# The last products of an encoder layer accumulate on banks that hold x and the gated sums

## The chip, the cores and the metric

The kernel runs on one core of one Trainium2 chip. The core has five engines with queues of their own: TensorE (PE, its weight loads PEld), VectorE (DVE), ScalarE (ACT), GpSimd (POOL) and SyncE (SP), which here only issues transfers. TensorE writes its results to PSUM, eight banks of 512 float32 columns by 128 partitions. The metric is the device time of one execution in microseconds, lower is better; runs are compared by their median.

## The reference

One layer of an encoder on 512 tokens of width 1024. After a norm and a projection to eight parts of 1024 columns there are a recurrent branch (convolution, two gated scans) and an attention branch over a neighbourhood of the token grid; both go through a projection, a gate each, and a sum. The end of the layer is what the change is about:

```python
merged = jax.nn.sigmoid(ga) * y_a + jax.nn.sigmoid(gb) * y_b
x = x + gate[:, None, :] * (merged @ w_o[l])
...
y = x32 * lax.rsqrt(jnp.mean(x32 * x32, axis=-1, keepdims=True) + EPS)   # rms_norm(x, g_final)
return (y * g.astype(jnp.float32)).astype(x.dtype)
```

`gate` is one row of 1024 numbers for all tokens, `w_o` is 1024 x 1024, and the output is float32.

## The kernel before

**Precision.** A float32 product is made of three TensorE products of a rounded high part and a low part (`mm3`: high by high, high by low, low by high), which accumulate in one bank. So each operand is split first: ScalarE writes the high part (`cast`, L411), VectorE subtracts it for the low part (`sub`, L414).

**The middle.** 72 main projections of 192 matmuls each (64 block products in three parts, 128x512 results called `acc`) follow each other on TensorE. Between their matmuls lie those of the attention (`sp`, `pt`, `pv`; VectorE makes `pp` from `pt` at L837, and `pv` multiplies `pp` by `vt`) and of the scans' gates (`gt`, 64 rows deep).

**The last stage.** `merged @ w_o` is done as a block product with seven instead of eight products (`ORDER`): merged is cut into quarters (token halves by halves of the inner dimension), `w_o` into the quarters 11, 12, 21, 22. Each product has sums of quarters on both sides: on the left `a11`, `a12`, `a22`, `s1` to `s4`; on the right 11, 21, 22 and `t1` to `t4` (`SUMS`; signs lie on the left side and in the sums afterwards). The inner half is four blocks of 128, so each product has for each of two token tiles t (0 and 1) 4 x 3 = 12 matmuls of 128x512, into a bank called `st`. The results are then combined: sums u1, u2, u3, and from them the four quarters of the output. A tile t of the upper half and tile t + 2 of the lower half share products; the output rows lie in `yo`, `y[t, n]` is the half row n of tile t. x is loaded into `yo` first.

Operations here before the change: the product 11 gives u1 (ScalarE copies the bank); u1 times gate is added to x in `yo`; u2 = u1 + t2's product, u3 = u2 + t3's; c22 and c12 from t1's; c21 = u3 + t4's; c12 + 22's product; each is multiplied by gate and added to `yo` (`mix`, L1131; sums with a bank at L1288); the product 21, with the gate already in its right side, is added to `yo` at L1284. Then `part_done`: squares of `yo` with a row sum (ScalarE L1234, in the very last piece VectorE L1230), the row's sums (L1242, L1243), root (ScalarE L1248), v, reciprocal and a Newton step (VectorE L1249 to L1254), the product with `gfin` (L1237, VectorE or GpSimd) and with the row's factor (ScalarE L1264 for a whole row of 1024; in the last tile VectorE L1258 and ScalarE L1261 for a half each), and the stores (L1265, L1260, L1262).

**Staging of w_o.** The 28 right sides (7 sums, 4 inner blocks) are made while the projections run: SP loads one quarter's block into `wb` (L406), GpSimd issues transfers that add the other quarters (`woa`, L1200), ScalarE and VectorE split it, SP writes it to a buffer in DRAM (`wscr`, L1208), and in the last stage it is loaded again as `woh`. `POS` says for each of the 28 behind which projection this starts. For the sum 21 the block is loaded into `wr` instead and multiplied by gate before it is split.

**What sets the order.** Every instruction is recorded by `op` with an engine, or a choice of them, a cost, and a rank; a planner (`Plan`) then runs a list schedule with these costs, with slots for each pool of tiles and with a limit on live banks of each kind (`LIMITS`), and emits each engine's instructions in that order. At run time each engine goes strictly in its order and waits for semaphores. So a change of any rank, cost or position shifts the order elsewhere too.

Of the kernel before, what the change touches and what calls it, by code (L numbers as in the profile page):

```python
# [348 lines left out]
def layer(ctx, tc, x, x_t, cin, par, w_m, w_v, w_vt, w_in, w_blk, rpb, w_pa, w_pb, w_o, g_final, out):  # L349
# [17 lines left out]
    def T(name, dt=F32):  # L367
        return pl.tile("s", lambda i: sb.tile([P, S], dt, tag=f"s{i}", name=nm(name)))
# [47 lines left out]
    def mm(o, a, b, first, last):  # L416
        nc.tensor.matmul(o, a, b, start=first, stop=last)  # L417
# [771 lines left out]
    for k in range(4):  # L1189
        block = {f"{i}{j}": w_o[(k + 4 * i - 4) * P:(k + 4 * i - 3) * P, 512 * j - 512:512 * j] for i in (1, 2) for j in (1, 2)}  # L1190
        for j, (_, g) in enumerate(ORDER):
# [31 lines left out]
    def part_done(t, n, a, b, rank, o, last, final):  # L1223

        w = b - a
        yy = lambda: yo[t].ap[:, n * 512 + a:n * 512 + b]
        rows = slice(t * P, (t + 1) * P)
        ssq = C("ssq", 1, 10)
        if final and last:
            op("DVE", dve(w) + 0.08, lambda e: nc.vector.tensor_tensor_reduce(  # L1230
# [188 lines left out]
```

## Time and profile before

| | |
|---|---|
| runs | 550.95, 552.49, 550.82 us; median 550.95 |
| profiled execution | 549.81 us, its span 548.0 us, granted TensorE clock 0.996 |
| busy, share of the span | PE 537.1 us (98%), PEld 447.0 (82%), DVE 419.7 (77%), ACT 343.4 (63%), POOL 131.4 (24%) |
| transfers | 132.35 MB, 241 GB/s over the span |
| the chain that ended last | PE 92%, DVE 4%, DMA 2% |

A line of the timeline gives start, duration, engine, source line, operation, output <- inputs, shape and count; in brackets stands how long the engine had been idle and what ended that. Neighbouring instructions of one kind are put together in one line, with their count. The duration of a matmul is longer than the distance to the next, because matmuls are pipelined. A line of the groups gives source line, engine, operation, names, shape and count, then total busy time and mean of one in ns, then the idle time before them. A line of the waits says who waited for whom, the sum, how often, and the longest.

### The profile page before, as it was taken

How to read it: one execution, taken by the hardware profiler on the slowest of the kernel's cores; microseconds unless marked ns; L12 is line 12 of the kernel's file. 1: busy time of each engine (PE TensorE's matmuls, PEld its weight loads, DVE VectorE, ACT ScalarE, POOL GpSimd, SP SyncE). 2: the span in 40 equal slices, each digit the busy share in tenths (PEclk: the TensorE clock that was granted, in tenths of full speed). 3: DMA queues.
4: the chain of work that ended last, by engine and by line, in shares of the span. 5: the costliest groups of instructions: out<-in, count | busy, mean ns of one | idle time of the engine just before them, and what ended most of it. 6: DMA issues, size and time to landing. Idle time of an engine off the chain costs nothing.

```text
span 548.0 us, 7826 instructions
## 1 busy us (share of the span) xinstructions
PE 537.1 (98%) x2684; PEld 447.0 (82%) x2684; DVE 419.7 (77%) x772; ACT 343.4 (63%) x614; POOL 131.4 (24%) x100
## 2 busy tenths in 40 slices
PE   9999999999999999999999999999999999999993
PEld 8888888888888888887887888888788888888882
DVE  5679518898788789888768988986974884688486
ACT  5578645854864755776986984996698535334044
POOL 3528656444433534220000000000002011000052
PEclk9999999999999999999999999999999999999998
DMA  8999999888976794487173174232319979999933
GB/s 329 408 409 407 368 343 332 227 309 254 253 238 241 189 317 125 126 198 221 43 306 135 39 225 158 98 109 85 115 45 320 303 228 282 348 390 415 413 154 154
DMA packets 48544, 132.35 MB, mean 241 GB/s; under 512 B 6512, under 2 KB 9720, under 8 KB 48504
## 3 DMA queue, kind: packets, MB, share of 16 engines
q1 hardware_dynamic: 44168, 124.18, 63.2%
q0 software_dynamic: 4032, 7.34, 7.7%
q8 instruction: 21, 0.34, 0.3%
q10 hardware_dynamic: 304, 0.33, 0.2%
q14 instruction: 19, 0.16, 0.1%
HBM read 110.69 MB, written 21.14 MB: 241 GB/s over the span
## 4 chain that ended last, share of the span: by engine, by line
PE 92%; DVE 4%; DMA 2%; ACT 0%; SPq 0%; issue 0%; DVEq 0%; ACTq 0%
PE acc L417 70%; PE hx L417 8%; PE st L417 5%; PE pv L417 2%; PE gt L417 2%; PE sp L417 2%; PE pt L827 2%; DMA rcx<-rscr 2%; DVE v L1249 1%; DVE yo L1131 1%; PE hx L526 1%; SPq L406 0%; PE mi L463 0%; DVE u L1131 0%; DVE u L1288 0%
## 5 line engine op out<-in xcount | busy, mean ns | idle before, releaser
L417 PE MATMUL acc<-hhl,whi 128*128 128x512 f32 x784 | 242.9, 391 | 0.0
L417 PEld LDWEIGHTS acc<-hhl,whi 128*128 128x128 f32 x784 | 145.8, 188 | 29.9 <-issue 0.4
L417 PE MATMUL acc<-hhl,wlo 128*128 128x512 f32 x392 | 152.7, 390 | 0.0
L417 PEld LDWEIGHTS acc<-hhl,wlo 128*128 128x128 f32 x392 | 73.6, 188 | 15.5
L1200 POOL DMA_DIRECT2D wb<-in_w_o_dram x28 | 24.4, 879 | 257.1 <-DMA wb<-in_w_o_dram 222.5
L414 POOL TENSOR_TENSOR wlo<-wraw,whi 128x1024 fp32r<-128x1024 f32 x27 | 67.6, 2512 | 74.1 <-ACT whi L411 58.2
L411 ACT CAST whi<-wraw 128x1024 fp32r<-128x1024 f32 x72 | 74.6, 1046 | 7.6 <-DMA wraw<-in_w_in_dram 4.5
L414 DVE TENSOR_TENSOR wlo<-wraw,whi 128x1024 fp32r<-128x1024 f32 x45 | 55.4, 1233 | 5.9 <-ACT whi L411 5.6
L417 PE MATMUL acc<-yahl,whi 128*128 128x512 f32 x128 | 39.4, 389 | 0.0
L417 PE MATMUL acc<-ybhl,whi 128*128 128x512 f32 x128 | 39.4, 389 | 0.0
L816 ACT ACTIVATE p<-p,mn 128x192 f32<-128x192 f32 (+1 forms) x64 | 30.4, 478 | 6.3 <-DVE mn L809 6.2
L809 DVE CUSTOM_DVE_ANT_0 p<-sp,nb 128x192 f32<-128x192 f32 (+1 forms) x64 | 31.0, 603 | 0.4
L417 PEld LDWEIGHTS acc<-ybhl,whi 128*128 128x128 f32 x128 | 24.0, 188 | 5.0
L417 PEld LDWEIGHTS acc<-yahl,whi 128*128 128x128 f32 x128 | 24.0, 188 | 5.0
L969 DVE SCALAR_TENSOR_TENSOR xc<-acc,prm,xc 128x511 f32<-128x511 f32 (+1 forms) x24 | 18.0, 749 | 12.3 <-ACT xc L962 11.8
L1063 DVE SCALAR_TENSOR_TENSOR gm<-gm,acc 128x512 f32<-128x512 f32 x16 | 11.0, 687 | 21.1 <-PE acc L417 21.1
L417 PE MATMUL acc<-ybhl,wlo 128*128 128x512 f32 x64 | 24.9, 389 | 0.0
L417 PE MATMUL acc<-yahl,wlo 128*128 128x512 f32 x64 | 24.9, 389 | 0.0
L1058 ACT ACTIVATE gm<-acc 128x512 f32<-128x512 f32 x16 | 9.6, 598 | 24.4 <-PE acc L417 24.3
L417 PE MATMUL hx<-vhl,xhl 128*128 128x512 f32 x96 | 24.3, 391 | 0.2 <-ACT xhl L567 0.2
L414 DVE TENSOR_TENSOR wb<-wb 128x512 fp32r<-128x512 f32 x24 | 20.4, 864 | 4.6 <-ACT wb L411 4.6
L996 ACT ACTIVATE ri<-gt,hb 64x512 f32<-64x512 f32 x32 | 21.9, 685 | 1.8 <-PE gt L417 1.2
(207 smaller groups left out, 1011.0 us busy)
## 6 DMA issues: line engine op xcount, KB each, us to landing
wraw<-in_w_in_dram SPq DMA_DIRECT2D x56, 512.0 KB
wscr<-wb SPq DMA_DIRECT2D x28, 512.0 KB
woh<-wscr SPq DMA_DIRECT2D x28, 512.0 KB
wc<-in_w_m_dram SPq DMA_DIRECT2D x24, 512.0 KB
wb<-in_w_o_dram POOLq DMA_DIRECT2D x28, 256.0 KB, 7.0
wb<-in_w_o_dram SPq DMA_DIRECT2D x24, 256.0 KB
vt<-vscr SPq DMA_DIRECT2D x20, 256.0 KB
wv<-in_w_v_dram SPq DMA_DIRECT2D x8, 512.0 KB
```

The lines of the kernel that those rows point to most:

```text
L411: return lambda e: nc.scalar.copy(o(), i()) if e == "ACT" else nc.vector.tensor_copy(o(), i())
L414: return lambda e: ENGINE[e].tensor_tensor(o(), a(), b().bitcast(F32), op=ALU.subtract)
L417: nc.tensor.matmul(o, a, b, start=first, stop=last)
L526: op("PE", 0.43, lambda e: nc.tensor.matmul(wb.ap[:, :P], warmc.ap, warmc.ap, start=True, stop=True), 5000 + j, r=[warmc], hold=[wb], unti ...
L809: nc.vector.tensor_tensor_reduce(out=o, in0=v(spv(h, e)[:, :nk]), in1=v(nb[:, h, :nk]), scale=-1.0, scalar=3e38, op0=ALU.add, op1=ALU.min, ...
L816: nc.scalar.activation(pv2(i), pv2(i), AF.Exp, bias=mn.ap[:, c:c + 1], scale=-1.0, accum_out=sm.ap[:, 4 * h + b:4 * h + b + 1])
L827: nc.tensor.transpose(ptp.ap[:, j * P:(j + 1) * P], pt_.ap[:, j * P:(j + 1) * P], ident.ap)
L969: nc.vector.scalar_tensor_tensor(a, b, wcol, a, op0=ALU.mult, op1=ALU.add)
L996: nc.scalar.activation(ri[2 * d].ap[H[e], :], bk[e].ap[H[e], :], AF.Tanh, bias=hb.ap[H[e], c:c + 1], scale=0.5)
L1058: op("ACT", act(512), lambda e: nc.scalar.activation(t.ap, o.ap, AF.Tanh, scale=0.5), n - 1.9, r=[o], w=[t], name="gm")
L1063: op("DVE", dve(512), lambda e: nc.vector.scalar_tensor_tensor(t.ap, t.ap, 1.0, o.ap, op0=ALU.add, op1=ALU.mult), n - 1.9, r=[o], rw=[t], ...
L1200: op("POOL", 1.1, lambda e, l=l, q=q, block=block: nc.gpsimd.dma_start(f32(l)(), block[q], accum_op=ALU.add), m0 + 2, rw=[l], late=6.0, fa ...
```

## The change

It changes the following, nothing else of what the kernel computes:

- **Banks that hold the rest of the sum.** Each tile keeps three banks through the last stage. On the first, the product 11 is copied out (u1) and gated into `v`; VectorE then writes v + x into the bank, and the product 21 accumulates on it (`start=False`, `on`). On the second, t2's product: VectorE adds u1 into the bank, ScalarE copies it out as u2, t3's product accumulates on it, ScalarE copies that as u3, VectorE gates it and writes gated + x into the bank, t4's product accumulates. On the third, t1's: c22 and c12 are read from it, c12 is gated, VectorE writes gated + x into the bank, 22's product accumulates. Only the half row of c22 is finished in `yo`.
- **Squares and scale read the bank.** `square` reads the bank (or `yo` for c22), `scaled` multiplies bank, row factor and `gfin` in one VectorE operation into `yo`. GpSimd keeps only the two products u times gate (c22) in this stage.
- **Gate in 12 operands.** The right sides 21, 22 and t4 are all multiplied by gate while they are staged (12 blocks instead of 4; all in `wr`, where the quarters are also added).
- **Order.** `SEQ` gives the order of the 14 products (number of the product in `ORDER`, plus 7 for tile 1), the last one is whole; `POS` is new; reloads are ranked by `SEQ`; x is loaded some projections sooner; `st` may have eight banks instead of six.

```diff
+SEQ = [0, 7, 9, 2, 8, 6, 1, 10, 3, 4, 12, 5, 11, 13]
+GATED = {"21": 0, "22": 1, "t4": 0}
-LIMITS = {"st": 6, ...
+LIMITS = {"st": 8, ...
...
-    def mm(o, a, b, first, last):
-        nc.tensor.matmul(o, a, b, start=first, stop=last)
+    def mm(o, a, b, first, last, on=False):
+        nc.tensor.matmul(o, a, b, start=first, stop=last, skip_group_check=on)
...
-            raw = T("wr") if g == "21" else None
+            raw = T("wr") if g in GATED else None
...
-            if g == "21":
-                op(EITHER, both(512), lambda e, raw=raw: mix(e, whole(raw), whole(raw), whole(gate[0]), ALU.mult), m0 + 1.5, r=[gate[0]], rw=[raw], lock=True,
+            if raw:
+                gr = gate[GATED[g]]
+                op(EITHER, both(512), lambda e, raw=raw, gr=gr: mix(e, whole(raw), whole(raw), whole(gr), ALU.mult), m0 + LOWR - 0.1 + 0.5 * len(more), r=[gr], rw=[raw], lock=True,
...
-        load(yo[t], whole(yo[t]), x[t * P:(t + 1) * P, :], n1 + 0.2 * t, 524288, after=gate_of(n1, 1), spare=1, name="xr")
+        load(yo[t], whole(yo[t]), x[t * P:(t + 1) * P, :], n1 - 3 + 0.7 * t, 524288, after=gate_of(n1, 3), spare=1, name="xr")
...
+        op("ACT", act(512, 0, True), lambda e: nc.scalar.activation(to.ap, o.ap, AF.Square, accum_out=ssq.ap), rank,
...
+        op("DVE", dve2(512) if 0 else dve(512), lambda e: nc.vector.scalar_tensor_tensor(y[t, n].ap, o.ap, rs.ap, gfin[n].ap, op0=ALU.mult, op1=ALU.mult),
...
+    first_of = {"11": 0, "t2": 1, "t3": 1, "t4": 1, "t1": 2, "22": 2, "21": 0}
+    turns = [(int(c) % 7, int(c) // 7) for c in SEQ]
...
+        grow = (t, first_of[sb_]) in banks
+        o = banks.setdefault((t, first_of[sb_]), None) or B("st")
...
+                mm3(o.ap, ah.ap[:, ts], al.ap[:, ts], bh.ap, bl.ap, k == 0 and not grow, k == 3, grow)
...
+        if sb_ == "11":
+            us[t], v = kept("u1"), T("v")
+            two_of(v, o, gate[0], ALU.mult, "eg")
+            two_of(o, v, y[t, 0], ALU.add, "e0", 0.2)
+        elif sb_ == "t2":
+            two_of(o, us[t], o, ALU.add, "u2")
+            us[t] = kept("u2")
...
+            two_of(c12, c12, gate[1], ALU.mult, "eg", 0.1)
+            two_of(o, w, c12, ALU.add, "e0", 0.2)
...
+        elif sb_ == "t4":
+            part_done(t + 2, 0, o, rank, False)
```

**How it moves instructions.** Source lines below are those of each kernel; a number behind a name tells tiles of one name apart, and x3 are the three parts of one block product.

TensorE at the end of the program, before: the last matmuls of tile 1's product 21, whose second operand is the pair `mhl`. `st_5349` is the product 21 of tile 0, `st_5371` and `st_5390` are the two halves of tile 1.

```order
L417 MATMUL st_5349<-woh_5199,mhl_5040 128x512 x3
L417 MATMUL st_5349<-woh_5209,mhl_5092 128x512 x3
L417 MATMUL st_5371<-woh_5183,mhl_4936 128x256 x3
L417 MATMUL st_5371<-woh_5192,mhl_4978 128x256 x3
L417 MATMUL st_5371<-woh_5199,mhl_5040 128x256 x3
L417 MATMUL st_5371<-woh_5209,mhl_5092 128x256 x3
L417 MATMUL st_5390<-woh_5183,mhl_4936 128x256 x3
```

TensorE at the same place in the new order: `st_5150` is the second bank of tile 1 (t4's product), `st_5122` its first bank, on which 21's product accumulates.

```order
L419 MATMUL st_5150<-woh_5143,mhl_5003 128x512 x3
L419 MATMUL st_5150<-woh_5157,mhl_5057 128x512 x3
L419 MATMUL st_5150<-woh_5168,mhl_5109 128x512 x3
L419 MATMUL st_5122<-woh_5019,mhl_4951 128x512 x3
L419 MATMUL st_5122<-woh_5044,mhl_5003 128x512 x3
L419 MATMUL st_5122<-woh_5262,mhl_5057 128x512 x3
L419 MATMUL st_5122<-woh_5055,mhl_5109 128x512 x3
```

Behind it: one group of 24 half-wide matmuls has become one of 12 whole ones, into a bank that already holds v + x, and t4's product of the same tile is now the one before it.

VectorE at the end of the program, before: `yo_5065` is the row block of tile 1, the names with 128x1 are the row's numbers.

```order
L1284 TENSOR_TENSOR yo_5065<-yo_5065,st_5371 128x256
L1243 TENSOR_SCALAR ssp_5418<-ssq_5406 128x1
L1237 TENSOR_TENSOR yo_5065<-yo_5065,gfin_4301 128x512
L1242 TENSOR_TENSOR ssp_5424<-ssp_5418,ssq_5420 128x1
L1284 TENSOR_TENSOR yo_5065<-yo_5065,st_5390 128x256
L1230 ISA junk_5428,ssq_5427<-yo_5065 128x256
L1230 ISA ssq_5427 128x1
L1249 TENSOR_TENSOR v_1063_5431<-ssq_5427,ssp_5424 128x1
L1250 RECIPROCAL r_1065_5435<-sd_1064_5433 128x1
L1253 SCALAR_TENSOR_TENSOR q_1066_5437<-r_1065_5435,v_1063_5431 128x1
L1254 SCALAR_TENSOR_TENSOR rs_1067_5438<-q_1066_5437,r_1065_5435 128x1
L1258 SCALAR_TENSOR_TENSOR yo_5065<-yo_5065,rs_1067_5438,gfin_4297 128x512
```

VectorE at the same place in the new order: `yo_5071` is the row block of tile 3, `yo_4957` that of tile 1.

```order
L1236 SCALAR_TENSOR_TENSOR yo_4943<-st_5091,rs_1054_5381,gfin_4592 128x512
L1255 TENSOR_TENSOR v_1057_5396<-ssq_5388,ssp_5305 128x1
L1256 RECIPROCAL r_1058_5402<-sd_1056_5394 128x1
L1259 SCALAR_TENSOR_TENSOR q_1059_5404<-r_1058_5402,v_1057_5396 128x1
L1260 SCALAR_TENSOR_TENSOR rs_1060_5405<-q_1059_5404,r_1058_5402 128x1
L1236 SCALAR_TENSOR_TENSOR yo_5071<-st_5150,rs_1060_5405,gfin_4592 128x512
L1236 SCALAR_TENSOR_TENSOR yo_5071<-yo_5071,rs_1060_5405,gfin_4698 128x512
L1255 TENSOR_TENSOR v_1063_5418<-ssq_5413,ssp_5336 128x1
L1256 RECIPROCAL r_1064_5420<-sd_1062_5416 128x1
L1259 SCALAR_TENSOR_TENSOR q_1065_5422<-r_1064_5420,v_1063_5418 128x1
L1260 SCALAR_TENSOR_TENSOR rs_1066_5423<-q_1065_5422,r_1064_5420 128x1
L1236 SCALAR_TENSOR_TENSOR yo_4957<-st_5122,rs_1066_5423,gfin_4592 128x512
```

Behind it: the two adds from a bank (L1284), the square (L1230) and the product with `gfin` (L1237) are gone from this place; the last operation takes the bank `st_5122` directly, and ahead of the last row's numbers stand the two scales of tile 3.

TensorE at a group of `pv` matmuls near 117 us of the profile, before:

```order
L417 MATMUL acc_1296<-hhl_722,whi_1020 128x512 x2
L417 MATMUL acc_1296<-hhl_722,wlo_1030 128x512
L417 MATMUL acc_1296<-hhl_712,whi_1020 128x512 x2
L417 MATMUL acc_1296<-hhl_712,wlo_1030 128x512
L417 MATMUL pv_1343<-pp_1293,vt_757 128x256
L417 MATMUL pv_1343<-pp_1293,vt_764 128x256
L417 MATMUL pv_1344<-pp_1293,vt_757 128x256
L417 MATMUL pv_1344<-pp_1293,vt_764 128x256
L417 MATMUL pv_1343<-pp_1318,vt_764 128x256
L417 MATMUL pv_1343<-pp_1318,vt_771 128x256
```

The same group in the new order, where `acc_1347` is the projection behind `acc_1297`:

```order
L419 MATMUL acc_1297<-hhl_712,whi_1020 128x512 x2
L419 MATMUL acc_1297<-hhl_712,wlo_1030 128x512
L419 MATMUL acc_1297<-hhl_736,whi_1020 128x512 x2
L419 MATMUL acc_1297<-hhl_736,wlo_1030 128x512
L419 MATMUL acc_1347<-hh_602,whi_1103 128x512
L419 MATMUL acc_1347<-hl_618,whi_1103 128x512
L419 MATMUL acc_1347<-hh_602,wlo_1129 128x512
L419 MATMUL pv_1358<-pp_1295,vt_757 128x256
L419 MATMUL pv_1358<-pp_1295,vt_764 128x256
L419 MATMUL pv_1359<-pp_1295,vt_757 128x256
L419 MATMUL pv_1359<-pp_1295,vt_764 128x256
```

What moved: `pv` stands three block rows later, behind `hhl_736` of its own projection and the first three matmuls of the next; six more matmuls of 512 columns lie ahead of it.

TensorE at the first group of gate matmuls (`gt`), near 252 us of the profile, before:

```order
L417 MATMUL gt_2913<-xl_2771,gwh_2421 128x512
L417 MATMUL gt_2912<-xh_2664,gwl_2451 128x512
L417 MATMUL gt_2913<-xh_2664,gwl_2451 128x512
L417 MATMUL pv_2924<-pp_2886,vt_2172 128x256
L417 MATMUL pv_2924<-pp_2886,vt_2181 128x256
L417 MATMUL pv_2925<-pp_2886,vt_2172 128x256
L417 MATMUL pv_2925<-pp_2886,vt_2181 128x256
L417 MATMUL pv_2924<-pp_2891,vt_2181 128x256
L417 MATMUL pv_2924<-pp_2891,vt_2186 128x256
L417 MATMUL pv_2925<-pp_2891,vt_2181 128x256
L417 MATMUL pv_2925<-pp_2891,vt_2186 128x256
L417 MATMUL gt_2941<-xh_2664,gwh_2421 128x512
```

The same place in the new order:

```order
L419 MATMUL acc_2881<-hhl_712,wlo_2678 128x512
L419 MATMUL acc_2881<-hhl_736,whi_2663 128x512 x2
L419 MATMUL acc_2881<-hhl_736,wlo_2678 128x512
L419 MATMUL gt_2940<-xh_2676,gwh_2424 128x512
L419 MATMUL gt_2941<-xh_2676,gwh_2424 128x512
L419 MATMUL gt_2940<-xl_2703,gwh_2424 128x512
L419 MATMUL gt_2941<-xl_2703,gwh_2424 128x512
L419 MATMUL gt_2940<-xh_2676,gwl_2455 128x512
L419 MATMUL gt_2941<-xh_2676,gwl_2455 128x512
L419 MATMUL gt_2954<-xh_2676,gwh_2424 128x512
```

What moved: `pv` no longer lies inside the group (it stands 12 matmuls of `acc` sooner), and all 24 `gt` matmuls of this group follow each other, where before they came as 6, then 8 of `pv`, 12, then 9 of `acc`, and 6. The next groups are whole in both orders, except for the fourth: 24 in a row before, and now 18, then 18 of `acc`, and 6.

More of the change, by code (lines that the diff above doesn't have):

```diff
@@ L1218, in layer @@
         y[t, 0], y[t, 1] = two_in(yo[t])
-        load(yo[t], whole(yo[t]), x[t * P:(t + 1) * P, :], n1 + 0.2 * t, 524288, after=gate_of(n1, 1), spare=1, name="xr")
+        load(yo[t], whole(yo[t]), x[t * P:(t + 1) * P, :], n1 - 3 + 0.7 * t, 524288, after=gate_of(n1, 3), spare=1, name="xr")
     junk = T("junk")
     ssum = {}
-    def part_done(t, n, a, b, rank, o, last, final):
-        w = b - a
-        yy = lambda: yo[t].ap[:, n * 512 + a:n * 512 + b]
-        rows = slice(t * P, (t + 1) * P)
-        ssq = C("ssq", 1, 10)
-        if final and last:
-            op("DVE", dve(w) + 0.08, lambda e: nc.vector.tensor_tensor_reduce(
-                out=junk.ap[:, :w], in0=yy(), in1=yy(), scale=1.0, scalar=0.0, op0=ALU.mult, op1=ALU.add, accum_out=ssq.ap), rank,
-               r=[y[t, n]], w=[ssq, junk], lock=True)
-        else:
-            op("ACT", act(w, 0, True), lambda e: nc.scalar.activation(o.ap[:, :w], yy(), AF.Square, accum_out=ssq.ap), rank,
-               r=[y[t, n]], rw=[o], w=[ssq])
-            if not final or n:
-                op(ANY, any_(w), lambda e: ENGINE[e].tensor_tensor(yy(), yy(), gfin[n].ap[:, a:b], op=ALU.mult),
-                   rank + 0.1, r=[gfin[n]], rw=[y[t, n]], lock=True, name="e2")
-        if not last:
-            p = ssum.get(t)
-            ssum[t] = q = C("ssp", 1, 10)
-            op("DVE", 0.16, (lambda e: nc.vector.tensor_tensor(q.ap, p.ap, ssq.ap, op=ALU.add)) if p else
-               (lambda e: nc.vector.tensor_scalar(q.ap, ssq.ap, D * EPS, None, op0=ALU.add)), rank, r=[ssq] + [p] * bool(p), w=[q])
@@ new lines, in square, with scaled @@
+    def square(t, n, o, rank):
+        ssq = C("ssq", 1, 10)
+        to = junk if o is y[t, n] else y[t, n]
+        op("ACT", act(512, 0, True), lambda e: nc.scalar.activation(to.ap, o.ap, AF.Square, accum_out=ssq.ap), rank,
+           r=[o], w=[ssq] + [to] * (to is junk), rw=[to] * (to is not junk), name="sqy")
+        return ssq
+    def scaled(t, n, o, rs, rank):
+        op("DVE", dve2(512) if 0 else dve(512), lambda e: nc.vector.scalar_tensor_tensor(y[t, n].ap, o.ap, rs.ap, gfin[n].ap, op0=ALU.mult, op1=ALU.mult),
+           rank, r=[rs, gfin[n]] + [o] * (o is not y[t, n]), rw=[y[t, n]], lock=o is y[t, n], name="out")
@@ new lines, in part_done @@
+    def part_done(t, n, o, rank, final):
+        rows = slice(t * P, (t + 1) * P)
+        ssq = square(t, n, o, rank)
+        if t not in ssum:
+            q = C("ssp", 1, 10)
+            op("DVE", 0.16, lambda e: nc.vector.tensor_scalar(q.ap, ssq.ap, D * EPS, None, op0=ALU.add), rank, r=[ssq], w=[q], lock=True)
+            ssum[t] = q, o
+            if final:
+                op("DVE", dve(512), lambda e: nc.vector.tensor_tensor(y[t, n].ap, o.ap, gfin[n].ap, op=ALU.mult), rank + 0.1,
+                   r=[o, gfin[n]], rw=[y[t, n]], name="e2")
@@ L1252, in newton @@
+        op("DVE", 0.17, lambda e: nc.vector.reciprocal(r.ap, sd.ap), rank, r=[sd], w=[r], lock=True)
         def newton(e):
```

130 lines of the change are left out of this document (57 added, 73 removed).

## The prediction

> **What bounds the kernel now.** I read the stretches first, then TensorE's waits, then the end in order of time. One line of the stretches is: from and to in us, length, busy time of PE, PEld, DVE, ACT and POOL (with instructions), granted clock, DMA share, GB/s. The cuts are at 8.6 us (start-up over), 500.5 us (first matmul of the last product) and 539 us (last matmul).
>
> ```profile
> 8.60:500.50 491.90, 491.23 (x2456) 407.83 (x2457) 383.89 (x693) 324.07 (x576) 118.14 (x83) 1.00 0.72 239
> 500.50:539.00 38.50, 38.41 (x181) 32.11 (x179) 28.31 (x53) 11.75 (x25) 9.43 (x7) 1.00 0.74 299
> 539.00:548.00 9.00, 0.00 (x0) 0.00 (x0) 4.40 (x16) 2.83 (x7) 0.65 (x1) 0.77 0.30 117
> ...
> PE hx L526 <- DVE warmc L435: 1.1, 1, 1.1
> PE pv L417 <- DVE pp L837: 0.5, 1, 0.5
> PE hx L417 <- ACT xhl L567: 0.2, 1, 0.2
> ```
>
> TensorE bounds it: busy 491.23 of 491.90 us and 38.41 of 38.50 at full clock. Its only waits are the last three lines, and one of them, 0.5 us for pp, lies where the change moves instructions. So time can come from three places: work that TensorE drops, that wait, and the 9.00 us after TensorE's last matmul. Everything that is taken off VectorE before 539 is worth nothing by itself; it is worth what it takes off the end. The end, in order of time:
>
> ```profile
> 533.16 5.75 PE L417 MATMUL st<-woh,mhl 128*128 128x512 f32 x36
> ...
> 537.39 1.13 DVE L1131 TENSOR_TENSOR yo<-yo,u 128x512 f32<-128x512 f32 x1
> 538.31 1.34 POOL L1237 TENSOR_TENSOR yo<-yo,gfin 128x512 f32<-128x512 f32 x1 [0.34 <-ACT st L1234]
> 538.44 1.23 DVE L1249 TENSOR_TENSOR v<-ssq,ssp 128x1 f32<-128x1 f32 x1
> 538.55 0.60 ACT L1234 ACTIVATE st<-yo 128x512 f32<-128x512 f32 x1
> 539.09 0.19 ACT L1234 ACTIVATION_READ_ACCUMULATOR st<-yo 128x1 f32 x1
> ...
> 540.11 0.41 DVE L1284 TENSOR_TENSOR yo<-yo,st 128x256 f32<-128x256 f32 x1
> ...
> 541.17 0.41 DVE L1284 TENSOR_TENSOR yo<-yo,st 128x256 f32<-128x256 f32 x1
> 541.62 0.42 DVE L1230 CUSTOM_DVE_ANT_0 junk<-yo 128x256 f32<-128x256 f32 x1
> ...
> 542.09 0.16 DVE L1249 TENSOR_TENSOR v<-ssq,ssp 128x1 f32<-128x1 f32 x1
> 542.09 0.29 ACT L1248 ACTIVATE sd<-ssq,ssp 128x1 f32<-128x1 f32 x1
> 542.42 0.16 DVE L1250 RECIPROCAL r<-sd 128x1 f32<-128x1 f32 x1 [0.17 <-ACT sd L1248]
> ...
> 543.06 0.75 DVE L1258 SCALAR_TENSOR_TENSOR yo<-yo,rs,gfin 128x512 f32<-128x512 f32 x1
> ...
> 543.84 0.33 SPq L1260 DMA_DIRECT2D out_dram<-yo  x1
> ```
>
> TensorE ends at 533.16 + 5.75 = 538.91, but the add of its last half starts at 541.17: VectorE is 2.26 us late. It was made late by its queue of 512-wide adds, and by GpSimd: the tiny v took 1.23 us beside a GpSimd product and 0.16 alone, an add took 1.13. After the add come the squares, the root, the scale (543.06), the store (543.84) and 4.16 us to the span's end at 548.0.
>
> **Part 1, the end.** Removed: the adds of x, of the gated sums and of the product behind the last matmuls; the bank then holds the finished row, ScalarE squares it there, VectorE scales it from there. Also the last product is one of 512 columns instead of two of 256. Prices:
>
> ```profile
> 522.28 5.60 PE L417 MATMUL st<-woh,mhl 128*128 128x512 f32 x24
> ...
> 527.72 5.60 PE L417 MATMUL st<-woh,s 128*128 128x512 f32 x24
> 527.92 0.69 DVE L1288 TENSOR_TENSOR u<-u,st 128x512 f32<-128x512 f32 x1 [0.80 <-PE st L417]
> ...
> 538.04 0.19 ACT L1234 ACTIVATION_READ_ACCUMULATOR st<-yo 128x1 f32 x1
> 538.26 0.29 ACT L1248 ACTIVATE sd<-ssq,ssp 128x1 f32<-128x1 f32 x1
> ...
> L1288 DVE TENSOR_TENSOR u<-u,st 128x512 f32<-128x512 f32 x8 | 5.5, 683 | 4.6 <-PE st L417 4.6
> L1131 DVE TENSOR_TENSOR u<-u,gate 128x512 f32<-128x512 f32 x4 | 2.8, 690 | 0.1
> L1234 ACT ACTIVATE st<-yo 128x512 f32<-128x512 f32 x7 | 4.2, 600 | 22.5 <-DVE yo L1131 21.1 <-DVE yo L1284 1.3
> L411 ACT COPY u<-st 128x512 f32<-128x512 f32 x2 | 1.2, 589 | 1.8 <-PE st L417 1.8
> ```
>
> - Matmuls of 512 columns follow each other every (527.72 - 522.28) / 24 = 0.227 us. The last 36 (12 whole, 24 halves) took 5.75; as 24 whole ones they take 5.60: TensorE ends 0.15 sooner, at 538.76.
> - VectorE began 0.04 after a group's end (522.28 + 5.60 = 527.88, then 527.92). ScalarE's square so starts at 538.80. Square and read-out take 539.09 + 0.19 - 538.55 = 0.73, the root follows 0.03 later (538.23 to 538.26): 539.56.
> - Root to scale is kept: 543.06 - 542.09 = 0.97, so the scale starts at 540.53. Scale to store is kept: 0.78, so 541.31. Store to end is kept, 4.16: **545.47 instead of 548.0, a gain of 2.53**.
>
> A square that reads a bank and writes SBUF has the nearest row in the copy out of a bank, 589 ns, against 600 for the square now; a scale that reads a bank has the add u<-u,st, 683 ns, against 690 without a bank. I take both as they are now. [...]
>
> Unknown is a VectorE write into a bank. Reading one costs nothing extra, so I take 0.69 as well; ScalarE's squares, which write into st, show no penalty either (600 against 589). Lower bound: no gain over 0.69. Upper: twice, 1.38. On the end's path there is none. The tightest place is the second product's chain: VectorE adds u into the bank (0.04 + 0.69), ScalarE copies it out (0.03 + 0.59), with some 0.3 for TensorE to see it: free 1.65 us after the product's last matmul, with 12 other matmuls, 2.72 us, in between. Doubled, 2.34: still covered. For the later banks (x and gated sums before the last products) the cover is 24 matmuls, 5.4 us, against four or five VectorE operations, 2.8 to 3.5 us; if all were doubled, 5.5 to 6.9, TensorE would wait up to 1.5 us. Value taken 0 (the rows nearest to it, a bank read and a bank written by ScalarE, both show none), range 0 to 1.5.
>
> On VectorE the scale of the row block that ends 12 matmuls earlier comes ahead of the last root's successor: it starts 0.04 + 0.73 + 0.03 + 0.97 = 1.77 after that product's end, two scales end by 3.3; the last reciprocal is wanted at 2.72 + 0.80 + 0.33 (542.09 to 542.42) = 3.85. Slack 0.5 us. GpSimd now has two operations in this stage instead of seven, so the stretching to 1.13 or 1.23 has no partner near the end.
>
> **Part 2, the wait for pp.** The order moves the eight pv matmuls behind six more 512-wide ones.
>
> ```profile
> 116.17 1.29 DVE L837 TENSOR_TENSOR pp<-pt,pp 128x512 fp32r<-128x512 f32 x2
> ...
> 117.01 1.25 PE L417 MATMUL pv<-pp,vt 128*128 128x256 f32 x8 [0.54 <-DVE pp L837]
> ```
>
> Six matmuls are 1.36 us, over the 0.54 waited, and VectorE's operations ahead of pp are the same ones: gain 0.5, between 0 (VectorE shifts with it) and 0.54. Elsewhere the cover of a pv group shrinks by three matmuls, 0.68 us; those groups did not wait.
>
> **Part 3, groups of gate matmuls.** They are 64 rows deep, and going into and out of them costs.
>
> ```profile
> 294.81 0.39 PE L417 MATMUL acc<-hhl,wlo 128*128 128x512 f32 x1
> 295.13 0.50 PE L417 MATMUL gt<-xh,gwh 64*128 64x512 f32 x2
> 295.46 0.40 PE L417 MATMUL gt<-xl,gwh 64*128 64x512 f32 x2
> 295.70 0.40 PE L417 MATMUL gt<-xh,gwl 64*128 64x512 f32 x2
> ```
>
> Going in: 0.32 instead of 0.227 to the first pair, and 0.33 instead of 0.24 to the second: 0.19 a switch. The first group is cut by pv and acc in the order before (six switches) and whole in the new one (two); the last is whole before and cut once in the new one (two more). Net two switches fewer: 0.38, between 0 and 0.76.
>
> **Part 4, what is added.** Eight more products of gate and operand on VectorE, 8 x 0.69 = 5.5 us, and eight blocks staged through another pool. VectorE is busy 383.89 of 491.90 us there, and TensorE waits for it once in the whole stretch; the products lie in the staging, whose results TensorE wants tens of us later. Cost 0 while that cover holds; if one comes ahead of a pp or a split that TensorE waits for, 0.69. The x loads now start some projections sooner, so they queue ahead of some reloads on SP; the x adds waited for them before, and that wait was not TensorE's. Cost 0, bounded by the rivals below.
>
> **Sum.** 2.53 + 0.5 + 0.38 = 3.4 us. The profiled execution took 549.81 us, so 546.4 on its basis (the 1.81 outside the span kept); the median of the runs is 550.95, 1.14 above it, so **547.5**.
>
> **Rivals.** The reloads decide these.
>
> ```profile
> 500.00:520.00 20.00, 20.00 (x89) 16.55 (x89) 11.42 (x23) 2.71 (x6) 0.00 (x0) 1.00 1.03 414
> ...
> 498.52 0.33 SPq L406 DMA_DIRECT2D yo<-in_x_dram x1
> 508.60 6.66 SPq L406 DMA_DIRECT2D woh<-wscr  x6
> ...
> 508.68 0.69 DVE L1131 TENSOR_TENSOR yo<-yo,v 128x512 f32<-128x512 f32 x1 [0.54 <-DMA yo<-in_x_dram]
> ```
>
> *Slower: the block staged last comes late.* The new order stages block (21, k=2) so late that its subtract stands on VectorE behind the add of u into the bank of the third product, and its store and reload follow. Counted from the stage's first matmul: 36 matmuls of 0.227, 8.16; add and subtract 0.04 + 0.69 + 0.69, issue 0.3: store at 9.9. An SP transfer issued at 498.52 was used at 508.68, 10.2 later, with the queue full (share 1.03): landed at 20.1. The reload is the last of the queue and takes another 5 (half, the queue running empty) to 10.2: 25.1 to 30.3. TensorE wants it after 129 matmuls, 29.2 (129 x 0.227). Margin 4.1 to -1.1. It decides when the two transfers take over 19.3 us together; one more round of the queue, 10.2, against the 4.1 leaves a wait of about 6: 6 - 3.4 = 2.6 lost, 553.6. For it: the full queue. Against: the margin, and a queue that drains as the stage goes on.
>
> *Same: one reload two places late.* Reloads leave SP every (6.66 - 0.33) / 5 = 1.27 us. If the new order needs one two places sooner than it comes, TensorE waits 2.5: 3.4 - 2.5 = 0.9 gained, 550.0. Against: no matmul of st waited for a transfer before.
>
> *Faster, but less: VectorE stays late.* If it is free only at 541.0 as now, the reciprocal starts there instead of at 539.9, and 1.1 of the 2.53 goes: 548.7. The extreme form, TensorE waiting 1.5 us for a bank, gives 549.0. [...]
>
> **How the numbers follow.** Forecast 0.70 (545.6, the profiled basis less 0.8, to 548.3, the median's basis plus 0.8; 0.8 is half of what the runs shown, 550.82 to 552.49, lie apart); VectorE late or a bank wait, 548.3 to 549.2, 0.12; one reload late, 549.3 to 552, 0.12; the last block late, over 552.6, 0.06. A change under 0.3%, 1.65 us, cannot be told here from none: so faster 0.82, same 0.12, slower 0.06. The range goes from 545.6 to 549.9.
>
> **What would show it.** Right: TensorE's only waits are the two at hx; its last matmul ends about 1 us sooner; the square starts within 0.1 of that; 6.7 us from TensorE's end to the span's end instead of 9.1; two GpSimd operations in the last stage. Wrong: a wait of an st matmul for woh, for a bank's ScalarE or VectorE writer, or for pp elsewhere; a VectorE operation on a bank of over 0.8 us; a reciprocal that starts later than the root's end.

## The result, and the profile after

| | before | changed | ratio, 95% interval |
|---|---|---|---|
| first comparison, median | 551.00 us (4 runs) | 545.97 us (4 runs) | 0.9906 [0.9885, 0.9926] |
| again, on one chip | 550.04 us (9 runs) | 546.07 us (5 runs) | 0.9925 [0.9913, 0.9938] |
| profiled execution (span) | 549.81 us (548.0) | 546.81 us (544.9) | |

The gain is 5.0 us by the first medians, 4.0 by the second, and 3.0 by the two profiled executions. The two profiled executions give less because of their start, which is no part of the change; that it also explains the microsecond between the two comparisons of medians is likely, but not shown. These are the timelines of before, of the changed kernel, and of its second profiled execution (the run "again" below), at the same instructions:

```profile
3.92 2.34 PE L463 MATMUL mi<-c,ident 128*128 128x128 f32 x16
...
8.72 0.74 PE L417 MATMUL hx<-vhl,xhl 128*128 128x512 f32 x2 [0.23 <-ACT xhl L567]
```

```profile
3.95 3.53 PE L465 MATMUL mi<-c,ident 128*128 128x128 f32 x16
...
9.91 0.73 PE L419 MATMUL hx<-vhl,xhl 128*128 128x512 f32 x2 [0.20 <-ACT xhl L569]
```

```profile
3.92 2.25 PE L465 MATMUL mi<-c,ident 128*128 128x128 f32 x16
...
8.79 0.73 PE L419 MATMUL hx<-vhl,xhl 128*128 128x512 f32 x2 [0.39 <-ACT xhl L569]
```

The same sixteen small matmuls took 2.34, 3.53 and 2.25 us, the last two in one and the same program. So I count from the first 128x512 `hx` matmul (8.72, 9.91, 8.79): from there to the span's end it is 539.28 us before, 534.99 and 535.01 us in the two executions of the changed kernel. **The change is worth 4.3 us.** Where they lie (read off the timelines, us from that first `hx` matmul; the `yb` groups are the projection matmuls that read `ybhl`, and the last column holds what was gained since the row above):

| place | before | changed | difference of the stretch |
|---|---|---|---|
| fourth `pt` group | 101.24 | 101.21 | 0.03 |
| fifth `pt` group | 128.26 | 127.39 | 0.84: the wait for `pp` |
| thirteenth `pt` group | 214.70 | 213.79 | 0.04 |
| first `yb` group | 253.68 | 251.88 | 0.89: the first gate group |
| third `yb` group | 347.15 | 345.35 | 0.00 |
| fourth `yb` group | 393.88 | 392.50 | -0.42: the last gate group |
| first `st` matmul | 491.80 | 490.42 | 0.00 |
| TensorE's end | 530.19 | 528.66 | 0.15: whole last product |
| the last store on SP | 535.12 | 531.18 | 2.41: the end |
| span's end | 539.28 | 534.99 | 0.35 |

The waits of TensorE after the change (who, for whom, sum, times, longest), and then its end in order of time:

```profile
PE hx L528 <- DVE warmc L437: 1.1, 1, 1.1
PE hx L419 <- ACT xhl L569: 0.2, 1, 0.2
...
533.65 4.92 PE L419 MATMUL st<-woh,mhl 128*128 128x512 f32 x21
...
538.18 0.75 DVE L1236 SCALAR_TENSOR_TENSOR yo<-st,rs,gfin 128x512 f32<-128x512 f32 x1
538.61 0.60 ACT L1230 ACTIVATE yo<-st 128x512 f32<-128x512 f32 x1 [1.70 <-PE st L419]
538.85 0.74 DVE L1236 SCALAR_TENSOR_TENSOR yo<-yo,rs,gfin 128x512 f32<-128x512 f32 x1
...
539.33 0.29 ACT L1254 ACTIVATE sd<-ssq,ssp 128x1 f32<-128x1 f32 x1
539.51 0.15 DVE L1255 TENSOR_TENSOR v<-ssq,ssp 128x1 f32<-128x1 f32 x1
539.66 0.17 DVE L1256 RECIPROCAL r<-sd 128x1 f32<-128x1 f32 x1
...
540.31 0.75 DVE L1236 SCALAR_TENSOR_TENSOR yo<-st,rs,gfin 128x512 f32<-128x512 f32 x1
...
541.09 0.33 SPq L1266 DMA_DIRECT2D out_dram<-yo  x1
```

The wait at `pv` is gone, and no `st` matmul waits for a bank or a reload. TensorE ends at 538.57, the square starts 0.04 later, straight from the bank, and the store is issued 2.52 us after TensorE's end instead of 4.93. VectorE has the scales of tile 3 until 539.59 and v until 539.66; the root is there at 539.62 and the reciprocal starts at 539.66: VectorE is in time by a hair.

What a VectorE write into a bank costs, for which the trace of before had no row (groups of the changed kernel from 500 us on, with the read of a bank beside them):

```profile
L1133 DVE TENSOR_TENSOR st<-v,yo 128x512 f32<-128x512 f32 x4 | 2.8, 700 | 0.1
L1133 DVE TENSOR_TENSOR v<-st,gate 128x512 f32<-128x512 f32 x4 | 2.8, 689 | 5.8 <-ACT u L413 5.8
...
L1133 DVE TENSOR_TENSOR st<-u,st 128x512 f32<-128x512 f32 x2 | 1.4, 696 | 1.5 <-PE st L419 1.4
```

700 ns into a bank, 689 out of one, 696 for both, against 690 for the product `u<-u,gate` without a bank before: 10 ns more at most, next to nothing, as taken. The scale from the bank took 0.75, as from SBUF before.

### The profile page after: what moved, and what is told of

Its sections match the earlier page's. It is cut to its first block, busy times and chain, and to the rows that moved or that the text cites. A ratio compares the mean times of both kernels' runs of the same rounds, so it can differ in the third digit from the quotient of the medians.

```text
span 544.9 us, 7821 instructions
## 1 busy us (share of the span) xinstructions
PE 537.3 (99%) x2672; PEld 447.4 (82%) x2672; DVE 418.2 (77%) x773; ACT 342.3 (63%) x615; POOL 124.0 (23%) x95
## 4 chain that ended last, share of the span: by engine, by line
PE 97%; DVE 2%; ACT 1%; issue 0%
PE acc L419 72%; PE hx L419 8%; PE st L419 6%; PE pv L419 3%; PE pt L829 2%; PE gt L419 2%; PE sp L419 2%; DVE yo L1236 1%; PE mi L465 1%; PE hx L528 1%; DVE wc L551 0%; ACT L1254 0%; DVE q L1259 0%; PE mi L521 0%; ACT yo L1230 0%; DVE rs L1260 0%
## 5 line engine op out<-in xcount | busy, mean ns | idle before, releaser
L1202 POOL DMA_DIRECT2D wr<-in_w_o_dram x12 | 11.0, 916 | 136.6 <-ACT whi L413 98.8
L1202 POOL DMA_DIRECT2D wb<-in_w_o_dram x16 | 14.4, 918 | 75.2 <-DMA wb<-in_w_o_dram 55.4
L1001 ACT ACTIVATE ri<-gt,hb 64x512 f32<-64x512 f32 x32 | 21.9, 686 | 1.6 <-DVE ri L1042 0.6
L998 ACT ACTIVATE ri<-gt,hb 64x512 f32<-64x512 f32 x32 | 21.9, 685 | 1.5 <-PE gt L419 0.9
```

The source lines that it names most:

```text
L998: nc.scalar.activation(ri[2 * d].ap[H[e], :], bk[e].ap[H[e], :], AF.Tanh, bias=hb.ap[H[e], c:c + 1], scale=0.5)
L1001: nc.scalar.activation(ri[2 * d + 1].ap[H[e], :], bk[e].ap[H[1 - e], :], AF.Tanh, bias=hb.ap[H[1 - e], c + 8:c + 9], scale=0.5)
L1202: op("POOL", 1.0, lambda e, l=l, q=q, block=block, raw=raw: nc.gpsimd.dma_start(raw.ap if raw else f32(l)(), block[q], accum_op=ALU.add), ...
```

## The experiments

Where the order is the same, the matmuls up to the last stage lie at the same place to 0.05 us from one execution to the next when counted from the first `hx` matmul, so small effects are read in that way; the times settle those of a microsecond or more. Two runs are exceptions: a shift of 0.28 us (the last add back on VectorE) and one of 0.51 us (plain pairs) came in the first 85 us and stayed.

**The changed kernel again** (no edit).

> The changed kernel once more, for the size of the gain and for the start. In the two profiles shown the first 128x512 hx matmul begins at 8.72 us before and at 9.91 us after, with the same instructions ahead of it, and the sixteen mi matmuls took 2.34 and 3.53 us. Theory: that is chance from one execution to the next and no part of the change; so this profile may begin at either time, the stretch from that first hx matmul to the end of TensorE's last matmul is 528.66 us again (within 0.1), and from there to the span's end 6.3 us (within 0.4). Over five rounds the gain comes out between 3.8 and 5.2 us. Rival: the later start belongs to the new program; then this profile begins at 9.9 again.

Measured: first `hx` matmul at 8.79, TensorE's end 528.66 after it, then 6.35 to the span's end; 546.07 against 550.04 us. The later start is not the program's. In the thirteen profiled executions of this study that first matmul lay between 8.72 and 9.97 us. In the two executions compared first, the sixteen `mi` matmuls begin 0.21 us apart at first and 0.11 us apart later, and the trace's record of the full TensorE clock begins where that changes: at 4.60 us before, and at 7.11 us in the changed kernel. The sixteen took 2.25 us here, with the first `hx` at 8.79; 3.53 in the changed kernel's first profile, with `hx` at 9.91; and 3.62 in the run with GpSimd put back (below), with `hx` at 9.97. What sets the point where the spacing changes was not shown.

### The end

**The last add back on VectorE.**

> The changed kernel with the very last product taken off its bank: product 21 of tile 1 goes to a bank of its own, VectorE adds v to x in SBUF earlier, and adds the product to it at the end; square and scale then read SBUF. The two other banks of each tile stay as changed. Theory: the add costs its own 0.69 and also the wait for VectorE, which is at the scales of tile 3 until 1.0 us after TensorE's last matmul; store at 2.52 + 0.69 + 1.0 = 4.2 us after TensorE's end instead of 2.52, time 1.7 us longer. Rival: VectorE is free there, only 0.7 us longer. Second rival: the last bank is all of the gain at the end, 2.4 us longer.

```diff
+        apart = final and sb_ == "21"
+        grow = grow and not apart
+        o = B("st") if apart else ...
-            two_of(o, v, y[t, 0], ALU.add, "e0", 0.2)
+            two_of(y[t, 0] if t == last_ else o, v, y[t, 0], ALU.add, "e0", 0.2)
...
+        elif apart:
+            two_of(y[t, 0], y[t, 0], o, ALU.add, "e1")
+            part_done(t, 0, y[t, 0], rank, final)
```

Its timeline, with TensorE's end at 532.83 + 4.92 = 537.75:

```profile
538.02 0.74 DVE L1236 SCALAR_TENSOR_TENSOR yo<-yo,rs,gfin 128x512 f32<-128x512 f32 x1
538.68 0.68 DVE L1133 TENSOR_TENSOR yo<-yo,st 128x512 f32<-128x512 f32 x1
...
541.90 0.33 SPq L1266 DMA_DIRECT2D out_dram<-yo  x1
```

547.74 us against 546.07 for the changed kernel on the same chip, 1.67 longer (against before 0.9957 [0.9944, 0.9971]); store 4.15 us after TensorE's end (1.7 and 4.2 expected). One add of 0.68 us costs 1.6 there, because it stands behind two scales of another tile. So only 0.68 of this part of the gain is the add's own time; the rest is that the last product needs VectorE only after the root.

**GpSimd out of the end of the kernel before**, in two forms. The first:

> The kernel before, leaving out the products with g_final of the tiles 0, 2 and 3 (five GpSimd operations of 1.3 to 1.6 us and one of VectorE), so that GpSimd stands idle beside VectorE at the end. Theory: VectorE was late by 2.26 us because GpSimd beside it stretched its operations (v to 1.23 instead of 0.16, an add to 1.13 instead of 0.69); without it the last half's add begins within 0.4 of TensorE's end, and the time is 1.9 to 2.2 us shorter. Rival: VectorE was late by the number of its own operations; then the add comes 0.7 sooner at most, and the time is 0 to 0.7 us shorter.

```diff
-            if not final or n:
+            if final and n:
                 op(ANY, any_(w), ... op=ALU.mult), rank + 0.1, ..., name="e2")
```

547.89 against 550.04 us, 0.9960 [0.9947, 0.9974]; the last half's add began 0.20 us after TensorE's end instead of 2.26. That fits the theory, but the planner filled the freed GpSimd with two adds and a product that had been VectorE's, so VectorE had less to do as well, and this run doesn't tell the two apart (the next expectation speaks of three adds; it was two adds and the product). Hence the second form, with the order of all other engines kept:

> The kernel before, with the five GpSimd products with g_final (tiles 0, 2, 3) not issued; every other engine has exactly the instructions and the order it had, which the run of the kernel without the products of these tiles had not (there the planner also gave GpSimd three adds of VectorE's). Theory, GpSimd beside VectorE stretched it: of the 2.26 us that the last half's add was late, 0.44 come back at the add of 1.13 us (537.39) and about 1.0 at the v of 1.23 us (538.44), and some 0.7 at the v of 0.84 us (532.79); the last add begins 0.1 to 0.6 after TensorE's end and the time is 1.6 to 2.2 us shorter. Rival: VectorE was late because of the number of its operations, and the gain of the other kernel came from the three adds; then the last add stays 1.5 us late or more, and the gain is 0.7 at most.

```diff
-                op(ANY, any_(w), lambda e: ENGINE[e].tensor_tensor(yy(), ...
+                op(ANY, any_(w), lambda e: e == "POOL" or ENGINE[e].tensor_tensor(yy(), ...
```

```profile
537.62 0.16 DVE L1249 TENSOR_TENSOR v<-ssq,ssp 128x1 f32<-128x1 f32 x1 [0.19 <-ACT st L1234]
...
539.54 0.41 DVE L1284 TENSOR_TENSOR yo<-yo,st 128x256 f32<-128x256 f32 x1
...
542.21 0.33 SPq L1260 DMA_DIRECT2D out_dram<-yo  x1
```

The v that took 1.23 us takes 0.16. TensorE ends at 538.96, the last add starts 0.58 later (2.26 before) and the store 3.25 (4.93): 1.68 us come back with nothing but GpSimd's products gone, so that much of the 2.41 was GpSimd's stretching of VectorE. Time 548.44 against 550.57 us, 0.9950 [0.9927, 0.9973].

**GpSimd put back beside the changed kernel's end.**

> The changed kernel with six more GpSimd operations in the tail: as soon as a half row of tile 2, 0 or 3 is finished, GpSimd multiplies it by g_final into a scratch tile that nobody reads. VectorE has nothing more to do. Theory (GpSimd beside VectorE stretches it): VectorE's scales of tile 0 and 3 take 1.2 to 1.4 instead of 0.75, and since the last reciprocal had only 0.05 us of slack behind them, the store comes 1 to 2.5 us later. Rival: the stretching was something else; then the tail is the same, 2.52 us from TensorE's end to the store, within 0.2.

```diff
+            for h in (n, 1 - n):
+                op("POOL", 0.01, lambda e, h=h: nc.gpsimd.tensor_tensor(spill.ap, y[t, h].ap, gfin[h].ap, op=ALU.mult), rank,
+                   r=[y[t, h], gfin[h]], w=[spill], name="more")
```

```profile
542.96 2.98 POOL L1273 TENSOR_TENSOR spill<-yo,gfin 128x512 f32<-128x512 f32 x2 [1.13 <-issue]
...
543.40 1.22 DVE L1255 TENSOR_TENSOR v<-ssq,ssp 128x1 f32<-128x1 f32 x1
544.55 0.15 DVE L1256 RECIPROCAL r<-sd 128x1 f32<-128x1 f32 x1
544.73 1.23 DVE L1259 SCALAR_TENSOR_TENSOR q<-r,v 128x1 f32<-128x1 f32 x1
546.00 0.16 DVE L1260 SCALAR_TENSOR_TENSOR rs<-q,r 128x1 f32<-128x1 f32 x1
...
546.97 0.33 SPq L1266 DMA_DIRECT2D out_dram<-yo  x1
```

551.93 us, slower than before (1.0031 [1.0012, 1.0050]): the store came 8.34 us after TensorE's end (538.63) instead of 2.52. The direction is that of the theory, the size was put at 1 to 2.5 and was 5.8, and the place was wrong: the long scales kept 0.75 (they mostly ran while GpSimd paused, 538.10 to 539.23 and 541.84 to 542.96); the one-number operations v and q grew to between 0.84 and 1.26, and q ended when GpSimd did (542.96 + 2.98 = 545.94). The trace of the kernel before shows which operations grew beside a GpSimd product and which did not:

```profile
536.33 1.64 POOL L1237 TENSOR_TENSOR yo<-yo,gfin 128x512 f32<-128x512 f32 x1 [2.70 <-DMA out_dram<-yo]
536.73 0.15 DVE L1243 TENSOR_SCALAR ssp<-ssq 128x1 f32<-128x1 f32 x1
536.80 0.68 DVE L1284 TENSOR_TENSOR yo<-yo,st 128x512 f32<-128x512 f32 x1
537.39 1.13 DVE L1131 TENSOR_TENSOR yo<-yo,u 128x512 f32<-128x512 f32 x1
```

Within one GpSimd product (536.33 to 537.97) an operation with one SBUF input (`ssp`) and an add with one SBUF input and a bank took 0.15 and 0.68, as in the run with GpSimd's products not issued; the next add, which reads two SBUF tiles, took 1.13 instead of 0.69 there and ended 0.55 behind GpSimd. In the run here the two that grew, v and q, also read two SBUF tiles. The rows of r and rs decide nothing: r started each time about half way through a pair of GpSimd products (536.67, 540.43, 544.55), and rs when the pair had ended (538.15, 541.88, 546.00 against 538.10, 541.84, 545.94). Why these grew and the others did not was not shown.

**The seven GpSimd operations on VectorE** in the kernel before.

> The kernel before with the seven GpSimd operations of the last stage on VectorE instead (nothing left out). It asks whether taking the work off GpSimd is enough, or whether the work has to go. Theory: without the stretching VectorE gains 1.7 us at the end (the run with the products not issued), but seven operations, 0.61 us apart, are 4.3 us more of its own, of which some 1.3 fall into idle time; the last half's add begins 2 to 3.5 us after TensorE's end (2.26 before), time 0 to 1.3 us longer. Rival: VectorE has room before the end for most of them; the add comes within 1 us, time 1 us shorter or more.

```diff
-    ANY = ("DVE", "POOL")
-    any_ = lambda n: (dve(n), pool_(n))
+    ANY = ("DVE",)
+    any_ = lambda n: (dve(n),)
```

```profile
542.30 0.41 DVE L1284 TENSOR_TENSOR yo<-yo,st 128x256 f32<-128x256 f32 x1
...
545.14 0.33 SPq L1260 DMA_DIRECT2D out_dram<-yo  x1
```

551.02 against 550.81 us, 1.0009 [1.0000, 1.0019]; the last add began 2.59 us after TensorE's end at 539.71. Taking the work off GpSimd alone was worth nothing here, with VectorE's order planned anew: it has to disappear from both, which is what adding on banks and scaling from them does.

### TensorE's order

**A wait removed and a group cut, on TensorE alone**, in the kernel before. The list that the planner gives was changed for TensorE after the planning, so that all other engines keep theirs (the remarks in this excerpt and the next are added here).

> The kernel before with TensorE's order alone altered at two places, every other engine as it was. First, the eight pv matmuls that waited 0.54 us for pp at 117 us come six acc matmuls later. Theory: the wait cost more than its row, 0.84 us, since TensorE starts slowly after it; first hx matmul to the fifth pt group 127.4 instead of 128.26 us. Rival: it cost the row's 0.54, 127.7. Second, the third group of gate matmuls (24 in a row) is cut into four by three matmuls of acc at each cut, six more switches. Theory: each costs 0.21; from the second to the third yb group (300.41 and 347.15 us from the first hx matmul before, 46.74 apart) it takes 48.0. Rival: only the 0.09 gap at a switch costs, 47.3. No rounds, since the two nearly cancel in the time.

```diff
+    pv = [i for i, t in enumerate(told) if t[0].name == "pv"]
+    ahead(told, pv[3], 2, r"p\d+")                 # two acc block rows ahead of the fourth pv
+    for n in (9, 10, 11):                          # one ahead of each further piece of the third gate group
+        g = [i for i, t in enumerate(told) if t[0].name == "gates"]
+        ahead(told, g[n], 1, r"p\d+")
```

The `pv` wait vanished from the list of waits, and from the fourth to the fifth `pt` group it took 26.18 us instead of 27.02: **0.84 for a wait whose row says 0.54**, as in the changed kernel. The other 0.30 can be read off the traces. The row counts idle time from the end of the matmul before, 0.39 after its start, while without a wait the next starts 0.23 after it: 0.16. And the eight `pv` matmuls behind the wait took 1.09 us up to the next `acc`, against 0.95 in the changed kernel: 0.14. In the cut group:

```profile
343.71 0.51 PE L443 MATMUL acc<-hh,whi 128*128 128x512 f32 x1 [1.47 <-ACT ri L1025]
...
344.61 0.50 PE L443 MATMUL gt<-xh,gwh 64*128 64x512 f32 x2
...
345.51 0.73 PE L443 MATMUL acc<-hhl,whi 128*128 128x512 f32 x2
...
346.41 0.50 PE L443 MATMUL gt<-xh,gwh 64*128 64x512 f32 x2
```

From one piece to the next, 344.61 to 346.41, it is 1.80 us for six `gt` and three `acc` matmuls, which take 0.70 and 0.68 inside their groups: 0.42 for two switches, 0.21 each, as expected. The whole stretch grew by 2.77 instead of 1.27, since the moved `acc` also waited 1.47 us for a bank (first row), which I had not foreseen. This wait, at a switch, cost 1.50, hardly more than its row. One run, 552.07 us.

**The last gate group whole**, in the changed kernel, in two ways.

> The changed kernel with TensorE's order altered at one place: the last group of gate matmuls is not cut (24 in a row; before that it was 18, then 18 of acc, then 6). Three pieces of it come 9 matmuls later than they did, one comes 9 sooner. Nothing else is moved on any engine. Theory (two switches between 64-row and 128-row matmuls fewer, 0.21 us each by the two profiles): first hx matmul to the end of the last matmul 528.24 instead of 528.66, a gain of 0.42, too small for the times. Rival: the pieces that come later make ScalarE and VectorE late, and a TensorE wait for one of them appears; then 0 to 2 us are lost.

> The changed kernel with the last group of gate matmuls whole at the place of its last piece (six block rows of acc are moved ahead of the first three pieces), every other engine as it was. In the other try one piece came sooner than before and waited 1.17 us for VectorE's read of the bank that it needed; here no piece comes sooner. Theory: two switches fewer, first hx matmul to TensorE's end 528.24 instead of 528.66, no wait; the time is 0.4 us shorter, below what five rounds can tell. Rival: three pieces come some 4 us later, ScalarE and VectorE behind them too, and a TensorE wait for a weight's low part appears; 0 to 2 us longer.

```diff
+    ahead(told, gates()[12], 3, r"p\d+")           # first form: three block rows ahead of the group,
+    g = gates()                                    # and its last piece right behind the third
+    told.insert(g[14] + 1, told.pop(g[15]))
...
+    ahead(told, gates[12], 6, r"p\d+")             # second form: six block rows ahead of the group
```

Timeline of the first and waits of the second:

```profile
392.44 0.63 PE L444 MATMUL gt<-xh,gwh 64*128 64x512 f32 x2 [1.17 <-DVE za L1038]
```

```profile
PE gt L442 <- ACT ri L1024: 0.6, 1, 0.6
```

Both theories fell. TensorE's end came at 529.82 and 529.31 us from the first `hx` matmul instead of 528.66, so 1.16 and 0.65 later; 547.27 us, 0.9948 [0.9936, 0.9961], and 546.59 us, 0.9929 [0.9915, 0.9942] against before. In both, a piece of the group waited until VectorE or ScalarE had read a bank, as the two rows say. The cut of the last group, which costs 0.42, is cheaper than either way around it that I tried.

### The price of what was added, and the order of the products

**Each gate product in the staging twice.**

> The changed kernel with each of its twelve gate products in the staging issued twice on VectorE (the operands then hold gate squared), twelve operations of 0.69 us more, at the same places in the order. Theory: they lie under the matmuls; first hx matmul to TensorE's end stays 528.66 us, within 0.1, except for the twelfth, which stands in the last stage in front of the add of u into a bank: that bank has 0.7 us of slack, so up to 0.2 us may appear there. Rival: VectorE is near its limit there, and each costs part of its 0.69: 1 to 8 us more, with waits of TensorE for VectorE.

```diff
-                op(EITHER, both(512), lambda e, raw=raw, gr=gr: mix(e, whole(raw), whole(raw), whole(gr), ALU.mult), ...
+                op(EITHER, both(512), lambda e, raw=raw, gr=gr: [mix(e, whole(raw), whole(raw), whole(gr), ALU.mult) for _ in range(2)], ...
```

TensorE's end 528.70 us from the first `hx` matmul, no wait besides the two at `hx`; 546.04 us in its one run. Twelve operations of 0.69 us more cost nothing, so the eight that the change adds are covered with room to spare, and the bank in the last stage had its slack.

**The block products in plain pairs.**

> The changed kernel with the block products of the last stage in plain pairs: 11 of both tiles, t2, t3, t1, t4, 22, 21 of both tiles. Theory: the order is no source of the gain. The cover between the writers of a bank and the next product stays 12 matmuls or more, TensorE does not wait, first hx matmul to TensorE's end stays 528.66 within 0.1; at the end the two scales of the tile before (now tile 0, whose last product is 12 matmuls earlier) stand at the same place on VectorE; time within 0.4 us of the changed kernel's. Rival: the written-out order is needed, and TensorE waits for a bank, for a reload, or VectorE's scales come too late; 0.5 to 3 us longer.

```diff
-SEQ = [0, 7, 9, 2, 8, 6, 1, 10, 3, 4, 12, 5, 11, 13]
+SEQ = [0, 7, 2, 9, 1, 8, 3, 10, 4, 11, 5, 12, 6, 13]
```

546.33 us, 0.9934 [0.9911, 0.9957], no wait of TensorE, the store 2.51 us after its end. The end came at 529.17 instead of 528.66, but all of the 0.51 had appeared 33 us after the first `hx` matmul, long before the last stage. The written-out order is not where the gain is. It even used up VectorE's slack at the end; in plain pairs VectorE waits for ScalarE before the last v and again before the reciprocal:

```profile
538.88 0.16 DVE L1255 TENSOR_TENSOR v<-ssq,ssp 128x1 f32<-128x1 f32 x1 [0.33 <-ACT yo L1230]
538.88 0.29 ACT L1254 ACTIVATE sd<-ssq,ssp 128x1 f32<-128x1 f32 x1
539.20 0.16 DVE L1256 RECIPROCAL r<-sd 128x1 f32<-128x1 f32 x1 [0.17 <-ACT sd L1254]
```

## Why the prediction was right, and where its terms were off

The forecast was 3.4 us, the same kernels by the trace show 4.3, and by the medians 5.0 and 4.0. The mechanism of the three parts was right, but the trace shows 0.9 more than their sum, 0.35 of it of unknown cause, and 545.97 lies only 0.4 above the lower end of the range. Point by point:

- *Part 1, the end, 2.53.* Measured 0.15 for the whole product, 2.41 from TensorE's end to the store (2.38 summed), and 0.35 more behind the store, which I had taken as kept. Of the mechanism, the runs show that 1.68 is GpSimd's stretching of VectorE (expected: about its size, since the rows of v and the add were read so) and that an add at that place would cost 1.6. The cause of the 0.35 stays open. From the last store to the span's end it was 3.80 to 3.88 us in all eight executions of the changed kernel and its variants, and in the two variants of the kernel before that have no GpSimd work at the end (not issued, or on VectorE); it was 4.16 to 4.25 us in the three others, the kernel before itself among them. The difference lies in the closing sequence of the program, where GpSimd's DRAIN instruction starts 3.50 us behind the store before and 3.26 after the change, and takes 0.23 and 0.10. GpSimd's late work alone doesn't make it: the changed kernel with GpSimd put back has 3.83.
- *Slack of 0.5 us on VectorE* was mis-sized: none was left, the reciprocal started as v ended. The sum took each tile's root as coming right behind its square, but the load of ScalarE's table, 1.28 us at 531.84, came ahead of the first root, and the chain that ended last runs from it through the scales of three tiles on VectorE without a pause. In plain pairs VectorE had been idle for 1.97 us before the v of the tile ahead, at 536.16, and had 0.50 us of idle time in the last tile (0.33 and 0.17). The missing slack cost nothing here, but what comes on top there shows: with GpSimd beside it the store came 5.8 us later.
- *Part 2, the wait for `pp`, 0.5.* Measured 0.84, outside of the bounds of 0 to 0.54. The step that failed was to take the wait's row as the price: another 0.16 lies between that row and the pace without a wait, and 0.14 in the matmuls that follow.
- *Part 3, gate groups, 0.38.* Measured 0.47: 0.89 gained at the first group, 0.42 lost at the last. 0.21 to 0.22 a switch, and 0.19 had been read; of the 0.42 for two switches in the cut group that leaves 0.23 for the return to 128 rows, a little more than for the entry.
- *Part 4, 0*: right, with the products doubled too.
- *VectorE's write into a bank, 0 of 0 to 1.5*: right, 700 ns. The 0.3 us for TensorE to see a bank come free was my estimate, and on the safe side: in the trace of before, the first `hx` started 0.05 us after ScalarE had made its operand (8.67 to 8.72) and `pv` 0.15 after VectorE's `pp` (116.86 to 117.01).
- *The late block.* Its store was issued 9.5 us after the stage's start (9.9 summed); from the store to the reload it took 7.5, and the reload was through long before it was needed. The first rows are SP's (store, then four reloads of which the last is issued at 517.49), the last is TensorE's first use:

```profile
510.02 0.32 SPq L1211 DMA_DIRECT2D wscr<-wb  x1
...
517.49 0.32 SPq L408 DMA_DIRECT2D woh<-wscr  x1
...
529.57 1.52 PE L419 MATMUL st<-woh,mhl 128*128 128x512 f32 x6
```

  In the stretches of the changed kernel (the last two numbers are the share of the DMA engines and GB/s) the transfers have stopped:

```profile
522.00:524.00 2.00, 2.00 (x11) 1.65 (x10) 1.93 (x3) 0.00 (x0) 1.00 (x1) 1.00 0.00 0
```

  So at least 7.5 us were left where the prediction had -1.1 to 4.1: the queue had run empty earlier than in the kernel before, whose share in the same two microseconds was 1.05.
- The other rivals didn't come: no reload late, no wait for a bank.
- *The basis.* Profiled execution and median stood 1.14 apart, which I had kept as it was. The start of an execution varies by as much (first `hx` at 8.72 to 9.97 us), and by chance the profile of before had an early start and that of the changed kernel a late one.

## What to carry to other kernels

When a last product must be added to something, let the accumulator hold that something beforehand, and read squares and scale from it: the engine that was late then isn't needed between the last matmul and the root (here the store came 2.52 instead of 4.93 us after TensorE's end). Look at the shortest operations beside GpSimd's long ones, not at busy shares: the one-number v that took 1.23 us beside a GpSimd product took 0.16 with those products not issued. And line up two traces at the first large matmul before differences of a few microseconds are read, since the start varied by 1.25 us here, more than some terms of the sum.

## What the runs showed of the hardware that I had not expected

A wait of TensorE in front of eight `pv` matmuls cost more than its row: 0.84 us for 0.54, in two kernels; one at a switch to 128 rows cost 1.50 for 1.47. A group of 64-row matmuls cost 0.42 us at its two ends together. One-number VectorE operations with two SBUF inputs took up to 1.26 us beside GpSimd's 128x512 products and 0.15 to 0.22 alone; six such GpSimd products, whose results nobody used, put the last store 5.8 us later.
